# A hybrid GLA/convolution layer whose seven-product matmuls are queued in one line: weights of two products ahead, another product order, two sums accumulated in PSUM

## The chip, the cores and the metric

One Trainium2 chip, one core of it. The metric is the device time of one execution in microseconds (us): median, lowest and highest of several runs. TensorE (PE) multiplies, VectorE (DVE) and ScalarE (ACT) work element by element, SyncE (SP) issues the DMAs; GpSimd (POOL) does next to nothing here.

## The reference, cut to what matters

```python
def hybrid_layer(h, g_pre, w_in, w_gate_up, b_gate, g_gla_out, w_conv, w_out, g_post):
    xn = rmsnorm(h, g_pre)                     # 16 meta tokens + 512, 2048 wide
    p = xn @ w_in
    q, k, v, z_gla, r, hc, gate_b, gate_c, z_conv = jnp.split(p, SPLIT_POINTS, axis=-1)
    log_a = log_sigmoid(r @ w_gate_up + b_gate) / GATE_TAU
    o = gla_chunked(heads(q) * DK ** -0.5, heads(k), heads(v), heads(log_a))   # 4 heads
    y_gla = rmsnorm(o, g_gla_out) * silu(z_gla)
    y_conv = gate_b * causal_dwconv(gate_c * hc, w_conv) * silu(z_conv)
    y = jnp.concatenate([y_gla, y_conv], axis=-1) @ w_out
    return h + rmsnorm(y, g_post)
```

All float32. `gla_chunked` needs, for each head, exponentials of a running sum of `log_a` along the tokens before its own small products can start.

## The kernel before

**Arithmetic.** `x @ w_in` is done with weight tiles of 128 output columns. A float32 operand is split in a high and a low part (`whi`, made by ACT at L117; `wlo = raw - whi`, made by DVE at L118; both in `split`, L113 to L119), and three matmuls, hi by hi, hi by lo and lo by hi, stand for one.

**Pairs and products.** Two weight tiles `na` and `nb` make a pair. Each is loaded in two halves of the 2048 rows: blocks 11 and 12 of `na`, 21 and 22 of `nb`, 512 KB each, into one of five `raw` buffers (`new_raw`, L121; `want`, L143). The 528 tokens are also cut in two halves of 264. The pair is then a 2 by 2 product of blocks, done with seven products P1 to P7 in place of eight (a Strassen-Winograd form). A product is 24 matmuls of 128 by 128 by 256 to 264 into one PSUM bank, written by `make` (L192): the split of its weight block, then the matmuls of L59. The weight blocks of P7, P6, P3 and P5 are sums that DVE makes first (`add`, L190, in place in a raw buffer). The token blocks of P1 to P7 are made once, in the prologue, by `combine` (L462) and `block` (L467 on ACT, L468 on DVE).

There are 25 pairs: z2z3, k1q1, v2v3, z4z5, k2q2, v4v5, z6z7, k3q3, v6v7, and then h0c0, b0s0 to h7c7, b7s7 for the convolution. `pair` (L221) writes one: for each product its split and matmuls, then what takes it out of PSUM, then `step(per)`, which runs some steps of the work in between. It has two forms. The one with `before` (the first three pairs) takes its products from `sums_first` (L202), in the order P7, P5, P6, P1, P2, P3, P4; the sum of P7 goes to one raw buffer more than the four blocks (`s3`, L208). The other uses P1, P2, P7, P6, P3, P5, P4. The results of a pair are sums of products: `q` and `f`, `u`, `v` are copies or partial sums in SBUF (L287, L298 on ACT; L303, L304, L308 on DVE), `put` and L313, L319 write the results.

**Work in between.** Generators queued in `left_over`: for each GLA head `decay` (L545: `log_a` from a small matmul `zp`, then on ACT exp, ln, and six exponentials, on DVE the running sum, L556), `gla_b` (L596), `gla_c` (L632), `gla_d` (L649) and `gla_e` (L670). After each z pair `silu` (L327) runs on ACT and a DMA writes `zd`.

**Stages.** Prologue (loads, `x` split, the plain matmuls of k0, q0, r, v0, v1, z0, z1; L345 to L507), in which the token blocks are made as their source tokens come free, and where the first five products of z2z3 are asked for (`got`, L497 to L506); the nine pairs with the GLA work; the 16 pairs of the convolution (L710); and the output product with norm and residual (L746 to L821).

**What sets the order.** The program text is not the order on an engine: a scheduler puts each engine's instructions in a fixed list when the kernel is built, and each engine works its list in order. Names such as `z2z3P` in the profile are PSUM banks of a pair's products. `ident`, `tpk`, `tpm` and `tpv` belong to small transposes of the GLA stage `gla_b`.

Of the kernel before, what the change touches and what calls it, by code (L numbers as in the profile page):

```python
# [41 lines left out]
def hymba_kernel(ctx, tc, xT, x, g_pre, w_r, w_t, w_up, b_gate, g_gla, w_conv, w_o, g_post, out):  # L42
# [98 lines left out]
    raws = {}  # L141

    def want(name):  # L143

        if name not in raws:
            i = TILE[name]
            raws[name] = []
            for g in range(2):
                r = new_raw()
                nc.sync.dma_start(r, w_t[i][:, NB * g:NB * g + NB, :])  # L150
                raws[name].append(r)

# [39 lines left out]
    def make(na, nb, name, raw, w):  # L192
        hi, lo = split(raw, [P, NB, P])
        (xh, xl), s = xc[name]
        pt = bank(f"{na}{nb}{name}")[:, 0:w]
        for k in range(NB):
            mm(pt, hi[:, k, :], xh[:, s, k, XHALF - w:], k == 0, False)
            mm(pt, hi[:, k, :], xl[:, s, k, XHALF - w:], False, False)
            mm(pt, lo[:, k, :], xh[:, s, k, XHALF - w:], False, k == NB - 1)
        return pt  # L200

    def sums_first(na, nb, w):  # L202

        want(na)
        want(nb)
        a11, a12 = raws.pop(na)
        a21, a22 = raws.pop(nb)
        s3 = new_raw()  # L208
        V.tensor_tensor(out=s3, in0=a11, in1=a21, op=ALU.add)
        yield make(na, nb, "P7", s3, w)  # L210
        add(a21, a22)
        yield make(na, nb, "P5", a21, w)
        add(s3, a22)
        yield make(na, nb, "P6", s3, w)
        yield make(na, nb, "P1", a11, w)
        yield make(na, nb, "P2", a12, w)
        add(a12, s3)
        yield make(na, nb, "P3", a12, w)
        yield make(na, nb, "P4", a22, w)

    def pair(na, nb, c0, dst_a, dst_b, nxt=(), stages=(), per=2, before=None, got=()):  # L221


        w = XHALF - c0

        def tmp(name):
            return ev.tile([P, XHALF], F32, name=name)[:, 0:w]

        def put(dst, in0, in1, op):
# [3 lines left out]
        if before is not None:  # L233
            left_over.extend(before)
            seq, got = got if got else (sums_first(na, nb, w), [])
            got = list(got)

            def get():
                return got.pop(0) if got else next(seq)

            p = get()
            u = tmp("u")
            A.copy(u, p)
            step(per)
            p = get()
            f = tmp("f")
            A.copy(f, p)
            step(per)
            p = get()
            v = tmp("v")  # L250
            V.tensor_tensor(out=v, in0=p, in1=u, op=ALU.subtract)
            step(1000)
            left_over.extend(stages)
            dst_a, dst_b = dst_a(), dst_b()
            p = get()
            q = tmp("q")
            A.copy(q, p)
            V.tensor_tensor(out=v, in0=v, in1=q, op=ALU.subtract)
            add(u, v)
            add(u, f)  # L260
            put(dst_b[1], v, f, ALU.add)
            step(per)
            p = get()
            put(dst_a[0], p, q, ALU.add)
            step(per)
            p = get()
            put(dst_a[1], p, u, ALU.subtract)
            step(per)
            for n in nxt:
                want(n)  # L270
            p = get()
            put(dst_b[0], v, p, ALU.subtract)
            step(1000)
            return

        left_over.extend(stages)
        want(na)
        want(nb)
        a11, a12 = raws.pop(na)
        a21, a22 = raws.pop(nb)  # L280

        def product(name, raw):
            return make(na, nb, name, raw, w)

        p = product("P1", a11)
        q = tmp("q")
        A.copy(q, p)  # L287
        step(per)
        p = product("P2", a12)
        dst_a, dst_b = dst_a(), dst_b()  # L290
        put(dst_a[0], p, q, ALU.add)
        step(per)
        for n in nxt:
            want(n)
        add(a11, a21)
        p = product("P7", a11)
        v = tmp("v")
        A.copy(v, p)  # L298
        step(per)
        add(a11, a22)  # L300
        p = product("P6", a11)
        u = tmp("u")
        V.tensor_tensor(out=u, in0=p, in1=q, op=ALU.subtract)  # L303
        V.tensor_tensor(out=v, in0=u, in1=v, op=ALU.subtract)  # L304
        step(per)
        add(a12, a11)
        p = product("P3", a12)
        V.tensor_tensor(out=u, in0=p, in1=u, op=ALU.subtract)  # L308
        step(per)
        add(a21, a22)  # L310
        p = product("P5", a21)
        for o, s, e in dst_a[1]:
            V.tensor_tensor(out=o, in0=u[:, s - c0:e - c0], in1=p[:, s - c0:e - c0],  # L313
                            op=ALU.subtract)
        put(dst_b[1], p, v, ALU.add)
        step(per)
        p = product("P4", a22)
        for o, s, e in dst_b[0]:
            V.tensor_tensor(out=o, in0=v[:, s - c0:e - c0], in1=p[:, s - c0:e - c0],  # L319
                            op=ALU.subtract)  # L320
        step(1000)
# [363 lines left out]
    def k_q(h, nxt, *stages, **kw):  # L685
        pair(f"k{h}", f"q{h}", 0, lambda: new_k(h), lambda: new_q(h), nxt, stages, **kw)

    def v_v(h, nxt, *stages, **kw):
        pair(f"v{2 * h}", f"v{2 * h + 1}", 0, lambda: new_v(2 * h), lambda: new_v(2 * h + 1), nxt,
             stages, **kw)  # L690

    def z_z(h, nxt, *stages, **kw):
        pair(f"z{2 * h}", f"z{2 * h + 1}", NM // 2, lambda: new_z(2 * h), lambda: new_z(2 * h + 1),
             nxt, stages, **kw)
        silu(2 * h, 2 * h + 1)
# [6 lines left out]
    v_v(2, ("z6", "z7"), gla_e(1), decay(2))
    z_z(3, ("k3", "q3"), gla_b(2), gla_c(2), gla_d(2))
    k_q(3, ("v6", "v7"), gla_e(2))
    v_v(3, ("h0", "c0"), decay(3))


    ycat = {}

    def conv(j, nxt, *stages):  # L710
        hh = g1.tile([P, L], F32, tag="kn", name="hh")[:, 0:S + 2]
        cc = g1.tile([P, L], F32, tag="qn", name="cc")[:, 0:S + 2]
        c0 = NM // 2 - 2

        def two(t):
            return ([(t[:, 0:S // 2 + 2], c0, XHALF)], [(t[:, S // 2 + 2:], NM // 2, XHALF)])

        pair(f"h{j}", f"c{j}", c0, lambda: two(hh), lambda: two(cc), (f"b{j}", f"s{j}"), stages[0])
        V.tensor_tensor(out=hh, in0=hh, in1=cc, op=ALU.mult)
        y = g1.tile([P, L], F32, tag="rr", name="y")[:, 0:S]  # L720
        A.activation(y, hh[:, 0:S], AF.Copy, scale=wc[:, j, 0:1])
        for i in (1, 2):
            V.scalar_tensor_tensor(out=y, in0=hh[:, i:i + S], scalar=wc[:, j, i:i + 1], in1=y,
                                   op0=ALU.mult, op1=ALU.add)
        bb = g1.tile([P, L], F32, tag="vt0", name="bb")[:, 0:S]
# [148 lines left out]
```

## Time and profile before

| | us |
|---|---|
| median of 3 runs | 852.63 |
| lowest, highest | 852.21, 853.37 |
| profiled execution, its own time | 851.39 |
| its span | 849.4 |
| PE busy in the span | 811.0 (95%) |
| DVE busy | 636.5 (75%) |
| ACT busy | 386.7 (46%) |
| mean granted PE clock | 0.985 |

The span is the time from the first to the last instruction that the profiler saw on the core; the profiled execution's own time is 2.0 us longer. Busy times of different engines overlap. A value in square brackets in a timeline row is how long the engine had been idle before that instruction, with what it waited for.

### The profile page before, as it was taken

What the parts mean: (1) busy time and instruction counts of PE and PEld (TensorE: products, weight loads), DVE (VectorE), ACT (ScalarE), POOL (GpSimd) and SP (SyncE); (2) the same over time, 40 slices, a digit from 0 to 9 for tenths busy, and PEclk for the clock granted to TensorE, in tenths of its full rate; (3) what the DMA queues carried; (4) which work ended last, traced back from release to release, by engine and by line L of the source; (5) the groups of instructions that cost most, each with busy time, mean ns of one, the idle gap of its engine ahead of it and who ended that gap; (6) DMA issues with size and microseconds to landing.
All of it is one profiled execution on the core that took longest, in us unless ns stands there. A gap on an engine that the chain in (4) does not pass through costs nothing.

```text
span 849.4 us, 14218 instructions
## 1 busy us (share of the span) xinstructions
PE 811.0 (95%) x5980; PEld 768.2 (90%) x5980; DVE 636.5 (75%) x823; ACT 386.7 (46%) x524; POOL 2.3 (0%) x14
## 2 busy tenths in 40 slices
PE   8999696998989999999999999999999899999996
PEld 8999696998989999999999999999999688888886
DVE  6999778789889889988888888888888814050433
ACT  7635463476473665444444444444444723140411
POOL 0000000000000000000000000000000000000000
PEclk9999898998999999999999999999999999999998
DMA  9522141323322351363332233333333615050154
GB/s 297 197 71 67 63 149 51 123 76 100 100 100 100 106 158 60 100 221 102 100 100 100 100 120 107 122 105 122 118 104 116 246 61 197 1 199 0 50 189 159
DMA packets 30560, 98.92 MB, mean 116 GB/s; under 512 B 3904, under 2 KB 4800, under 8 KB 29728
## 3 DMA queue, kind: packets, MB, share of 16 engines
q1 hardware_dynamic: 28912, 94.86, 33.8%
q10 hardware_dynamic: 1584, 3.15, 1.0%
q8 instruction: 47, 0.77, 0.4%
q14 instruction: 17, 0.14, 0.0%
HBM read 89.61 MB, written 8.39 MB: 115 GB/s over the span
## 4 chain that ended last, share of the span: by engine, by line
PE 80%; DVE 9%; ACT 7%; issue 2%; DMA 2%; SPq 0%; DVEq 0%; ACTq 0%
PE out L59 21%; PE v L59 3%; PE z L59 3%; PE z2z3P L59 2%; PE v2v3P L59 2%; PE h7c7P L59 2%; PE h5c5P L59 2%; PE h2c2P L59 2%; PE h6c6P L59 2%; PE h4c4P L59 2%; PE h3c3P L59 2%; PE h1c1P L59 2%; PE b3s3P L59 2%; PE b6s6P L59 2%; PE b5s5P L59 2%
## 5 line engine op out<-in xcount | busy, mean ns | idle before, releaser
L117 ACT CAST whi<-raw 128x1024 fp32r<-128x1024 f32 x207 | 216.5, 1050 | 231.8 <-DVE raw L190 47.5
L118 DVE TENSOR_TENSOR wlo<-raw,whi 128x1024 fp32r<-128x1024 f32 x207 | 250.7, 1221 | 46.2 <-ACT whi L117 45.8
L190 DVE TENSOR_TENSOR raw<-raw 128x1024 f32<-128x1024 f32 x97 | 118.3, 1221 | 2.9 <-DMA raw<-in_w_t_dram 1.4
L800 DVE TENSOR_TENSOR yg<-out,gpost 128x512 f32<-128x512 f32 (+1 forms) x17 | 11.2, 659 | 107.1 <-ACT junk L799 106.9
L799 ACT ACTIVATE junk<-out 128x512 f32<-128x512 f32 (+1 forms) x17 | 9.7, 572 | 117.5 <-PE out L59 117.5
L59 PE MATMUL out<-whi,ygh 128*128 128x512 f32 (+1 forms) x136 | 51.5, 382 | 2.5 <-ACT ygh L754 2.5
L59 PE MATMUL out<-whi,ygl 128*128 128x512 f32 (+1 forms) x136 | 52.0, 382 | 0.3 <-DVE ygl L755 0.3
L59 PE MATMUL out<-wlo,ygh 128*128 128x512 f32 (+1 forms) x136 | 51.9, 381 | 0.0
L59 PE MATMUL out<-whi,ych 128*128 128x512 f32 (+1 forms) x136 | 51.9, 381 | 0.0
L59 PE MATMUL out<-whi,ycl 128*128 128x512 f32 (+1 forms) x136 | 51.9, 381 | 0.0
L59 PE MATMUL out<-wlo,ych 128*128 128x512 f32 (+1 forms) x136 | 51.9, 381 | 0.0
L59 PEld LDWEIGHTS out<-whi,ygh 128*128 128x128 f32 x136 | 25.4, 188 | 8.1 <-ACT ygh L754 2.7
L59 PEld LDWEIGHTS out<-whi,ygl 128*128 128x128 f32 x136 | 25.5, 187 | 6.2 <-DVE ygl L755 0.8
L59 PEld LDWEIGHTS out<-wlo,ych 128*128 128x128 f32 x136 | 25.5, 188 | 5.5
L59 PEld LDWEIGHTS out<-wlo,ygh 128*128 128x128 f32 x136 | 25.5, 187 | 5.5
L59 PEld LDWEIGHTS out<-whi,ycl 128*128 128x128 f32 x136 | 25.5, 188 | 5.5
L59 PEld LDWEIGHTS out<-whi,ych 128*128 128x128 f32 x136 | 25.5, 187 | 5.5
L128 ACT CAST whi<-raw 128x1024 fp32r<-128x1024 f32 (+2 forms) x13 | 10.9, 845 | 20.4 <-PE v L59 9.6
L59 PE MATMUL z2z3P<-xt,whi 128*128 128x256 f32 x48 | 10.5, 318 | 7.5 <-ACT whi L117 7.5
L59 PEld LDWEIGHTS z2z3P<-xt,whi 128*128 128x128 f32 x48 | 8.7, 220 | 8.0 <-ACT whi L117 8.0
L59 PE MATMUL k1q1P<-xb,whi 128*128 128x264 f32 x32 | 7.2, 324 | 7.1 <-ACT whi L117 7.1
L59 PEld LDWEIGHTS k1q1P<-xb,whi 128*128 128x128 f32 x32 | 6.0, 226 | 7.3 <-ACT whi L117 7.3
(687 smaller groups left out, 2336.4 us busy)
## 6 DMA issues: line engine op xcount, KB each, us to landing
raw<-in_w_t_dram SPq DMA_DIRECT2D x108, 512.0 KB, 4.3
raw<-in_w_o_dram SPq DMA_DIRECT2D x32, 512.0 KB, 5.0
xres<-in_x_dram SPq DMA_DIRECT2D x4, 1024.0 KB, 6.1
xr<-in_xT_dram SPq DMA_DIRECT2D x7, 528.0 KB, 6.5
z<-zd SPq DMA_DIRECT2D x8, 256.0 KB, 3.2
yd<-z SPq DMA_DIRECT2D x8, 256.0 KB, 2.2
yg<-yd SPq DMA_DIRECT2D x1, 2048.0 KB, 9.6
out_dram<-yg SPq DMA_DIRECT2D x8, 256.0 KB, 2.5
```

The lines of the kernel that those rows point to most:

```text
L59: nc.tensor.matmul(out_, lhsT, rhs, start=start, stop=stop)
L117: A.copy(hi, raw)
L118: V.tensor_tensor(out=lo, in0=raw, in1=hi.bitcast(F32), op=ALU.subtract)
L128: A.copy(hi[:, k, :], raw[:, k, :])
L190: V.tensor_tensor(out=a, in0=a, in1=b, op=ALU.add)
L799: nc.scalar.activation(junk, pt, AF.Square, accum_out=s_)
L800: nc.vector.tensor_tensor(out=yg[:, t, cs], in0=pt, in1=gpost[:, cs], op=ALU.mult)
```

## The change

All 25 pairs are entered in one list, `line`, of 175 products, by a class `Pair`. Each product has three parts: `prepare` (the sum, the split, the loads of the next pair's blocks), `multiply` (the 24 matmuls) and `away` (what takes it out of PSUM). A loop at the end of the text prepares up to two products ahead of the one that it multiplies. The order is P5, P1, P6, P2, P3, P7, P4 for all pairs. P2 is added onto P1's bank and P3 onto P5's, by matmuls that go on accumulating, so that the bank name of P2's matmuls is now P1's, and that of P3's is P5's. ACT's copies `q` (of P1) and `f` (of P5) are taken before that; one result half is then copied by ACT (L265). The signs of some sums of blocks change, and P7's weight block is a difference (L213). No pair uses a fifth raw buffer any more. In the prologue the blocks are made in another order, and the first three products of z2z3 are multiplied between them. The GLA stages start at other products (`STAGE`, the letters d, t, s, o, g for `decay` and `gla_b` to `gla_e`): those in `stages` are queued when a pair's P2 is taken away, those in `before` at its P5.

```diff
-ORDER = ("P1", "P2", "P7", "P6", "P3", "P5", "P4")
+ORDER = ("P5", "P1", "P6", "P2", "P3", "P7", "P4")
+AHEAD = 2
...
+        def prepare(self, name, nxt):
+            for b in ("21", "22", "11", "12"):
+                self.load(b)
+            raw = self.raw
+            if name == "P5":
+                add(raw["21"], raw["22"])
+            elif name == "P6":
+                add(raw["11"], raw["21"])
+            elif name == "P3":
+                add(raw["12"], raw["11"])
+            elif name == "P7":
+                V.tensor_tensor(out=raw["11"], in0=raw["11"], in1=raw["22"], op=ALU.subtract)
+            b = {"P5": "21", "P1": "11", "P6": "11", "P2": "12", "P3": "12", "P7": "11",
+                 "P4": "22"}[name]
+            two = split(raw[b], [P, NB, P])
+            if nxt and name in ("P5", "P6", "P4"):
+                nxt.load({"P5": "21", "P6": "22", "P4": "11"}[name])
+                if name == "P4":
+                    nxt.load("12")
+            return two
+
+        def multiply(self, name, two):
...
+            bank_of = {"P2": "P1", "P3": "P5"}.get(name)
+            if bank_of:
+                pt = self.sb[bank_of]
...
+        def away(self, name):
+            sb = self.sb
+            if name == "P5":
+
+                left_over.extend(STAGE[g[0]](int(g[1])) for g in self.before)
+                A.copy(self.tmp("f"), sb["P5"])
+            elif name == "P1":
+
+                A.copy(self.tmp("q"), sb["P1"])
+            elif name == "P6":
+                V.tensor_tensor(out=self.tmp("u"), in0=sb["P6"], in1=sb["q"], op=ALU.subtract)
+            elif name == "P2":
...
+                left_over.extend(STAGE[g[0]](int(g[1])) for g in self.stages)
+                self.dst_a, self.dst_b = self.dst()
+                for o, s, e in self.dst_a[0]:
+                    A.copy(o, sb["P1"][:, s - self.c0:e - self.c0])
+            elif name == "P3":
+                self.put(self.dst_a[1], sb["P5"], sb["u"], ALU.subtract)
+            elif name == "P7":
+                v = self.tmp("v")
+                V.tensor_tensor(out=v, in0=sb["u"], in1=sb["P7"], op=ALU.subtract)
+                self.put(self.dst_b[1], v, sb["f"], ALU.subtract)
+            else:
+                self.put(self.dst_b[0], sb["v"], sb["P4"], ALU.subtract)
...
-    z_z(2, ("k2", "q2"), gla_e(0), decay(1))
-    k_q(2, ("v4", "v5"), gla_b(1), gla_c(1), gla_d(1))
...
+        z_z(2, stages=("g0", "d1"), per=3)
+        k_q(2, stages=("t1", "s1", "o1"), per=3)
...
-        order = sums_first("z2", "z3", XHALF - NM // 2)
-        got = [next(order)]
+        all_pairs()
+        prepare_next()
+        prepare_next()
         block("P1", xa, 0, b11)
-        got.append(next(order))
+        multiply(0)
+        prepare_next()
         block("P2", xb, 0, b21)
...
+    for n in range(len(line)):
+        while len(ready) < min(len(line), n + 1 + AHEAD):
+            prepare_next()
+        if n >= first:
+            multiply(n)
+        away(n)
```

Three places of the engines' lists. **DVE at the end of the prologue.** L402 (now L440) scales the last z tile; L468 (L506) makes low parts of token blocks; L209 and L190 (L183) make sums of weight blocks, L118 (L119) their low parts. Before:

```order
L402 TENSOR_TENSOR raw_886<-z10_901,rstd_109 128x256
L402 TENSOR_TENSOR raw_886<-z11_902,rstd_109 128x256
L468 TENSOR_TENSOR xb1_100<-xr_108,xb0_99 128x1056 x2
L209 TENSOR_TENSOR raw_1013<-raw_1005,raw_1009 128x1024
L190 TENSOR_TENSOR raw_1009<-raw_1009,raw_1011 128x1024
L118 TENSOR_TENSOR wlo_1016<-raw_1013,whi_1015 128x1024
L118 TENSOR_TENSOR wlo_1050<-raw_1009,whi_1049 128x1024
```

And of the change, where raw_1005 is the sum for P5, raw_1009 P1's block and then P6's sum, raw_1011 P2's block and then P3's sum:

```order
L183 TENSOR_TENSOR raw_1005<-raw_1005,raw_1007 128x1024
L506 TENSOR_TENSOR xa1_98<-tt_521,xa0_97 128x1056
L506 TENSOR_TENSOR xa1_98<-xr_108,xa0_97 128x1056
L119 TENSOR_TENSOR wlo_1015<-raw_1005,whi_1014 128x1024
L119 TENSOR_TENSOR wlo_1021<-raw_1009,whi_1020 128x1024
L506 TENSOR_TENSOR xb1_100<-xr_108,xb0_99 128x1056
L440 TENSOR_TENSOR raw_886<-z10_901,rstd_109 128x256
L440 TENSOR_TENSOR raw_886<-z11_902,rstd_109 128x256
L183 TENSOR_TENSOR raw_1009<-raw_1009,raw_1005 128x1024
...
L119 TENSOR_TENSOR wlo_1055<-raw_1009,whi_1054 128x1024
...
L183 TENSOR_TENSOR raw_1011<-raw_1011,raw_1009 128x1024
...
L119 TENSOR_TENSOR wlo_1124<-raw_1011,whi_1123 128x1024
```

The first sum and two low parts have moved ahead of the last z tile; before, the first sum came behind it and behind all the token blocks. (The rows left out are L506 behind raw_1009's sum; the low part of P2, wlo_1090, and L506 twice behind wlo_1055; and L506 behind raw_1011's sum.)

**PE, third to fifth product of z2z3** (change; whi_1054 is P6's weight block, whi_1123 P3's, whi_1089 P2's):

```order
L60 MATMUL z2z3P6_1093<-xt0_766,wlo_1055 128x256
L60 MATMUL z2z3P5_1028<-xb0_99,whi_1123 128x256
L60 MATMUL z2z3P5_1028<-xb1_100,whi_1123 128x256
L60 MATMUL z2z3P1_1064<-xb0_99,whi_1089 128x256
L60 MATMUL z2z3P1_1064<-xb1_100,whi_1089 128x256
L60 MATMUL z2z3P1_1064<-xb0_99,wlo_1090 128x256
```

Two matmuls of P3 stand ahead of all of P2; P3's other 22 follow P2.

**ACT in the decay of head 1.** Before (whi_2104 and whi_2140 are the weights of z4z5's P5 and P4, whi_2174 that of k2q2's P1):

```order
L554 ACTIVATE esx_1968<-esx_1968 128x528
L117 CAST whi_2104<-raw_1852 128x1024
L117 CAST whi_2140<-raw_1854 128x1024
L578 ACT_TABLE_LOAD
L578 ACTIVATE dec_2022<-B_1967 128x4
L573 ACTIVATE eqk_1969<-eqk_1969 128x512
L574 ACTIVATE eqk_1969<-eqk_1969,lns_76 128x512
L577 ACTIVATE esx_1968<-esx_1968 128x528
L575 ACTIVATE esx_1968<-esx_1968 128x512
L580 ACTIVATE B_1967<-B_1967,lns_76 128x512
L117 CAST whi_2174<-raw_1982 128x1024
```

And of the change (whi_2123 is k2q2's P1, whi_2166 its P6; z_2005 and z_2006 are z4 and z5, whose silu (L330) stood behind the whole decay before; ahead of these rows stand the two biased exps of L591, a table load, the exp of L595, the cast of k2q2's P5, a table load and the ln of L596):

```order
L300 ACT_TABLE_LOAD
L300 ACTIVATE z_2005<-z_2005 128x512
L118 CAST whi_2123<-raw_2041 128x1024
L620 ACT_TABLE_LOAD
L620 ACTIVATE dec_2074<-B_2026 128x4
...
L622 ACTIVATE B_2026<-B_2026,lns_76 128x512
L253 COPY f_2197<-k2q2P5_2172 128x264
L300 ACT_TABLE_LOAD
L300 ACTIVATE z_2006<-z_2006 128x512
L567 CAST ed0_2157<-B_2026 128x512
L256 COPY q_2228<-k2q2P1_2203 128x264
L118 CAST whi_2166<-raw_2041 128x1024
```

(Between the rows of L620 and L622 stand the same four exponentials as before, in another order.) Behind the exponentials stood the weights of k2q2's first product, P1; now those of its first two, P5 and P1, stand among them and those of its third, P6, behind, and the silu of z4 and of z5 has moved into the chain, each with a table load. The copy `q` of P1's bank stands ahead of P6's weights.

## Rows read from the trace of the kernel before

**Rows 1.** The page: share and count of busy time by engine; the 40 slices of PE and of the clock granted to it; shares of the chain that ended last by engine; the load of a weight block with its median time from issue to landing.

```profile
PE 811.0 (95%) x5980; PEld 768.2 (90%) x5980; DVE 636.5 (75%) x823; ACT 386.7 (46%) x524; POOL 2.3 (0%) x14
...
PE   8999696998989999999999999999999899999996
...
PEclk9999898998999999999999999999999999999998
...
PE 80%; DVE 9%; ACT 7%; issue 2%; DMA 2%; SPq 0%; DVEq 0%; ACTq 0%
...
raw<-in_w_t_dram SPq DMA_DIRECT2D x108, 512.0 KB, 4.3
```

**Rows 2.** The view of stretches, all engines: start and end in us, length, then busy us and (instructions) of PE, PEld, DVE, ACT and POOL, the granted clock, the DMA share and GB/s.

```profile
86.00:116.00 30.00, 22.50 (x175) 22.00 (x174) 24.04 (x27) 13.23 (x16) 0.53 (x1) 0.89 0.25 86
116.00:146.00 30.00, 22.47 (x169) 21.74 (x168) 22.86 (x36) 18.46 (x26) 0.00 (x0) 0.89 0.33 99
146.00:190.00 44.00, 44.00 (x366) 43.13 (x366) 35.81 (x53) 25.08 (x41) 0.00 (x0) 1.00 0.29 97
190.00:201.00 11.00, 6.65 (x37) 6.22 (x37) 9.86 (x18) 6.47 (x13) 0.00 (x0) 0.69 0.27 77
...
250.00:256.00 6.00, 3.14 (x22) 2.38 (x22) 6.00 (x14) 4.63 (x8) 0.00 (x0) 1.00 0.04 15
...
325.00:328.00 3.00, 1.38 (x12) 1.09 (x11) 3.00 (x6) 1.92 (x3) 0.00 (x0) 1.00 0.03 5
...
363.00:365.00 2.00, 0.74 (x7) 0.54 (x7) 1.86 (x6) 1.61 (x3) 0.00 (x0) 1.00 0.29 72
...
380.00:659.00 279.00, 279.00 (x2351) 279.00 (x2349) 238.98 (x286) 121.14 (x141) 0.00 (x0) 1.00 0.34 110
```

**Rows 3.** The waits of PE: what waited, for whom, total us, how often, the longest us.

```profile
PE z2z3P L59 <- ACT whi L117: 7.5, 2, 7.0
PE k1q1P L59 <- ACT whi L117: 7.1, 1, 7.1
PE k2q2P L59 <- ACT whi L117: 4.3, 1, 4.3
PE out L59 <- ACT ygh L754: 2.5, 1, 2.5
PE v6v7P L59 <- DVE wlo L118: 1.6, 1, 1.6
PE z6z7P L59 <- ACT whi L117: 1.5, 1, 1.5
PE v4v5P L59 <- DVE wlo L118: 1.4, 1, 1.4
PE ot L678 <- DVE on L665: 1.3, 1, 1.3
```

**Rows 4.** The view of stretches again (columns as in rows 2): the first microseconds of PE behind its three longest idle times, and one behind the wait of 2.5 us.

```profile
93.40:97.30 3.90, 3.38 (x14) 3.09 (x15) 3.62 (x4) 1.20 (x2) 0.00 (x0) 0.50 0.07 23
138.30:142.00 3.70, 3.55 (x14) 3.25 (x15) 3.40 (x3) 0.90 (x1) 0.00 (x0) 0.50 0.69 239
195.00:200.00 5.00, 4.96 (x23) 4.73 (x24) 4.79 (x6) 1.52 (x4) 0.00 (x0) 0.50 0.43 113
...
662.00:663.00 1.00, 0.96 (x4) 0.43 (x3) 1.00 (x2) 1.00 (x2) 0.00 (x0) 1.00 1.02 430
```

**Rows 5.** The timeline of DVE at the end of the prologue: start, us, line, operation, count, idle time before.

```profile
75.50 0.75 DVE L402 TENSOR_TENSOR raw<-z,rstd 128x256 f32<-128x256 f32 x2
76.16 2.42 DVE L462 TENSOR_TENSOR tt<-tt,xr 128x1056 f32<-128x1056 f32 x2
...
86.98 0.75 DVE L402 TENSOR_TENSOR raw<-z,rstd 128x256 f32<-128x256 f32 x2
87.65 2.42 DVE L468 TENSOR_TENSOR xb<-xr,xb 128x1056 fp32r<-128x1056 f32 x2
91.04 1.22 DVE L209 TENSOR_TENSOR raw<-raw 128x1024 f32<-128x1024 f32 x1 [0.98 <-DMA zd<-raw]
```

**Rows 6.** The timeline of ACT in the decay of head 1, columns as in rows 5.

```profile
181.74 0.85 ACT L549 ACTIVATE esx<-zp,bg 128x264 f32<-128x264 f32 x2
...
183.54 1.28 ACT L553 ACT_TABLE_LOAD   x1
184.84 0.65 ACT L553 ACTIVATE esx<-esx 128x528 f32<-128x528 f32 x1
185.39 0.35 ACT L298 COPY v<-z4z5P 128x256 f32<-128x256 f32 x1
...
191.67 0.72 ACT L574 ACTIVATE eqk<-eqk,lns 128x512 f32<-128x512 f32 x1
...
197.59 0.61 ACT L525 CAST ed<-B 128x512 fp32r<-128x512 f32 x1
```

**Rows 7.** Groups of instructions by line and form between 380 and 659 us: count, busy us, mean ns of one, idle time before them.

```profile
L118 DVE TENSOR_TENSOR wlo<-raw,whi 128x1024 fp32r<-128x1024 f32 x98 | 118.6, 1221 | 19.2 <-ACT whi L117 19.1
L304 DVE TENSOR_TENSOR v<-u,v 128x258 f32<-128x258 f32 x7 | 3.0, 429 | 0.7
...
L117 ACT CAST whi<-raw 128x1024 fp32r<-128x1024 f32 x98 | 103.1, 1052 | 136.7 <-DVE raw L190 18.6 <-PE h1c1P L59 8.5 <-PE b2s2P L59 8.4
L287 ACT COPY q<-h1c1P 128x258 f32<-128x258 f32 x1 | 0.4, 378 | 0.0
```

**Rows 8.** The chain that ended last, one pair of the convolution: start, us, what.

```profile
399.81 19.90 PE b1s1P L59 x168
```

More of the change, by code (lines that the diff above doesn't have):

```diff
@@ L139, in load_gran @@
         return gran
[L141 to L151, printed above, removed]
     def plain_k(pts, wt, kt, c0):
@@ L177, in hymba_kernel @@
     left_over = []
+    STAGE = {}
+    line = []
+    ready = []
     def step(n):
@@ L190, in add @@
         V.tensor_tensor(out=a, in0=a, in1=b, op=ALU.add)
[L192 to L229, printed above, removed]
+    class Pair:
+        def __init__(self, na, nb, c0, dst, done=None, stages=(), before=(), per=2):
+            self.na, self.nb, self.c0, self.w, self.dst = na, nb, c0, XHALF - c0, dst
+            self.done, self.stages, self.before, self.per = done, stages, before, per
+            self.raw, self.sb = {}, {}
+            for n, name in enumerate(ORDER):
+                line.append((self, n, name))
+        def load(self, b):
+            if b not in self.raw:
+                r = new_raw()
+                g = NB * (b in ("12", "22"))
+                i = TILE[self.na if b[0] == "1" else self.nb]
+                nc.sync.dma_start(r, w_t[i][:, g:g + NB, :])
+                self.raw[b] = r
+        def prepare(self, name, nxt):
[19 more added lines that the diff above has]
+        def multiply(self, name, two):
+            hi, lo = two
+            (xh, xl), s = xc[name]
+            c0, w = self.c0, self.w
+            bank_of = {"P2": "P1", "P3": "P5"}.get(name)
+            if bank_of:
+                pt = self.sb[bank_of]
+            else:
+                pt = bank(f"{self.na}{self.nb}{name}")[:, 0:w]
+                self.sb[name] = pt
+            kw = {"skip_group_check": True} if bank_of else {}
+            for k in range(NB):
+                mm(pt, hi[:, k, :], xh[:, s, k, c0:], k == 0 and not bank_of, False, **kw)
+                mm(pt, hi[:, k, :], xl[:, s, k, c0:], False, False, **kw)
+                mm(pt, lo[:, k, :], xh[:, s, k, c0:], False, k == NB - 1, **kw)
+        def tmp(self, name):
+            self.sb[name] = ev.tile([P, XHALF], F32, name=name)[:, 0:self.w]
+            return self.sb[name]
+        def put(self, dst, in0, in1, op):
+            c0 = self.c0
@@ L230, in put @@
             for o, s, e in dst:
                 V.tensor_tensor(out=o, in0=in0[:, s - c0:e - c0], in1=in1[:, s - c0:e - c0], op=op)
[L233 to L321, printed above, removed]
+        def away(self, name):
[8 more added lines that the diff above has]
+            elif name == "P2":
+                if self.before:
+                    step(1000)
+                left_over.extend(STAGE[g[0]](int(g[1])) for g in self.stages)
[8 more added lines that the diff above has]
+                self.put(self.dst_b[1], v, sb["f"], ALU.subtract)
+            else:
+                self.put(self.dst_b[0], sb["v"], sb["P4"], ALU.subtract)
@@ new lines, in prepare_next, with multiply, away @@
+    def prepare_next():
+        n = len(ready)
+        if n < len(line):
+            p, i, name = line[n]
+            at = line.index((p, 0, ORDER[0])) + len(ORDER)
+            ready.append(p.prepare(name, line[at][0] if at < len(line) else None))
+    def multiply(n):
+        p, i, name = line[n]
+        p.multiply(name, ready[n])
+    def away(n):
+        p, i, name = line[n]
+        p.away(name)
+        step(p.per if i < len(ORDER) - 1 else 1000)
+        if i == len(ORDER) - 1 and p.done:
+            p.done()
@@ L683, in gla_e @@
             yield
[L685 to L695, printed above, removed]
@@ L697, in hymba_kernel @@
-    z_z(1, ("k1", "q1"), before=(), got=(order, got))
-    k_q(1, ("v2", "v3"), before=(decay(0),), per=3)
-    v_v(1, ("z4", "z5"), gla_c(0), gla_d(0), before=(gla_b(0),))
-    z_z(2, ("k2", "q2"), gla_e(0), decay(1))
-    k_q(2, ("v4", "v5"), gla_b(1), gla_c(1), gla_d(1))
[L702 to L725, printed above, removed]
-        sg = g1.tile([P, L], F32, tag="vt1", name="sg")[:, 0:S]
-        pair(f"b{j}", f"s{j}", NM // 2, lambda: main_only(bb), lambda: main_only(sg), nxt, stages[1])
-        A.activation(sg, sg, AF.Silu)
-        V.tensor_tensor(out=y, in0=y, in1=bb, op=ALU.mult)
-        return y, sg
@@ L732, in conv_end @@
[L732 to L743 removed]
+    STAGE.update(d=decay, t=gla_b, s=gla_c, o=gla_d, g=gla_e)
```

90 lines of the change are left out of this document (67 added, 23 removed).

## The prediction, made before the changed kernel was run

> **What bounds the kernel now.** I read the page first: PE is busy for 811.0 of 849.4 us, and 80% of the chain that ended last is PE [rows 1]. So the end moves only by PE's idle time and by time at a low clock. The slices (21.2 us each) show where these are: the PE line falls to 6 in the fifth and seventh, to 8 in the tenth and twelfth, and the clock line falls to 8 in the fifth, seventh and tenth [rows 1]. The view of stretches gives sizes [rows 2]: PE is idle for 7.5 us in 86 to 116, 7.5 in 116 to 146, 4.35 in 190 to 201, 2.9 in 250 to 256, 1.6 in 325 to 328, 1.3 in 363 to 365; nothing in 146 to 190, and nothing at all in 380 to 659, the convolution, where DVE is busy for 239 of 279 us and never the limit. The waits name the cause [rows 3]: the first product of z2z3 waits for its weights behind the last z tile; k1q1, k2q2, v4v5 with z6z7, and v6v7 wait for weights which stand behind the decay of heads 0 to 3 in the lists of ACT and DVE. The last look is at the clock [rows 4]: behind the idle times of 7.0, 7.1 and 4.3 us TensorE ran at 1.2 GHz (0.50) for busy times of 3.38, 3.55 and 4.96 us, and half of each is lost against 2.4 GHz: 1.7 + 1.8 + 2.5 = 6.0 us. Behind the 2.5 us in front of the output product it stayed at 1.00 [rows 4].
>
> Before, the idle time that the change can touch is therefore 7.5 + 7.5 + 4.35 + 2.9 + 1.6 + 1.3 = 25.15 us, and 6.0 of clock: 31.2.
>
> **The change, part by part.** I walk each engine's list with durations of the rows. A product is 19.90 / 7 = 2.85 us of PE [rows 8]; a low part or a sum 1.22, pitched some 1.15 apart where they follow each other (two token blocks take 2.42) [rows 5, 7]; a cast 1.05, a copy out of PSUM 0.38 [rows 7].
>
> *Head.* Before, the first sum starts at 91.04, behind four token blocks, the z tile and a wait for the DMA that empties a buffer which it takes as fifth one [rows 5]; PE waits until 93.40 [rows 4]. Now the sum is made in place and stands two token blocks behind the two combines at 76.16 [rows 5]. From there six large instructions and some 0.8 us of waits for ACT's blocks give 84, and P5's low part 85: before the z matmuls end at 93.40 - 7.0 = 86.4 [rows 3, 4]. P5 and P1 start without a wait. DVE goes on: P1's low part to 86.1, a block, the z tile (0.75) to 88.0, P6's sum to 89.1, a block, P6's low part to 91.4; P6 is due at 86.4 + 5.7 = 92.1. Behind it PE's list has two matmuls of P3, ahead of P2. P3's sum comes behind P2's low part and two blocks, at 96.1, its cast at 97.2; P6 ends at 94.95. **A wait of 2.25 remains** of 7.5 + 1.7.
>
> *Decay of head 1.* The `zp` matmuls start the chain; ACT's list is then: two biased exps 0.74, table load 1.28, exp 0.65, cast 1.03, load 1.28, ln 0.65, load 1.28 and silu 0.63, cast 1.04, load 1.28, `dec`, the four exponentials and `B` 3.24, copy 0.37, load 1.28 and silu 0.63, `ed` 0.61, copy 0.37, cast of P6 1.04 [rows 6, 7]: 17.4, with a little DVE time 17.6. PE has five products ready behind `zp`: P3, P7, P4, then P5 and P1 of k2q2, 14.25 us. **Wait 3.4** where 4.35 and 2.5 of clock stood.
>
> *Decays of heads 2 and 3.* No silu stands in these chains, which come to 13.5; but the copy `q` of P1's bank stands ahead of P6's cast, so P6 cannot start before P1's end + 0.38 + 1.05 = 1.4. With the low part and the next block's cast behind it I get **2.8 and 2.75**, where 2.9 and 1.6 stood: nothing gained, 1.1 lost.
>
> *Decay of head 0.* It starts one product later than the others in its pair's order. The cast of v2v3's P5 stands at 14.6 + 0.8 (a wait for DVE's scan) behind `zp`, four products and four single matmuls cover 11.9. **Wait 3.5** (part of it ahead of P3's low part), where 7.5 and 1.8 stood.
>
> *Copies, sums in PSUM.* DVE loses some 50 instructions, about 0.4 us each [rows 7], ACT gains 23. In the convolution PE had no idle time [rows 2], so that is worth nothing there; it is hidden by PE. Without this cover it would be 20 us of DVE. Matmuls that add to a used bank are as many as before, of the same shape: 0. Gain or loss from them is bounded by nothing shown, except that in-bank accumulation is what all but the first of the 24 matmuls do already.
>
> *Bank.* P2 may write P1's bank only once ACT has copied `q`. P6 (2.85) lies between, the copy takes 0.38: ACT may be late by 2.4 before PE waits. *Loads.* The next pair's fourth block to be needed first is asked for at P6 and lands 4.3 us later [rows 1]; the next P5 is prepared three products, 8.5 us, after. Hidden.
>
> *A rule against the change.* ACT's next instruction starts 1.30 us after the table load's start (183.54, 184.84), and the copy at 185.39 overlaps the end of the exp [rows 6]: a switch costs its own row. The change puts two more switches into head 1's chain. The Trainium skill, "ScalarE: Activation LUTs", section "What ACT_TABLE_LOAD costs", says that a switch costs some 1380 ns of drain besides the 1283 ns load, and to keep functions of one set together. By that, five loads would make the chain 6.9 us longer and head 1's wait 10.3; the trace shows the load of 1.28 and no drain, so the sum goes by the row.
>
> **Sum.** After: 2.25 + 3.5 + 3.4 + 2.8 + 2.75 + 1.3 (`ot`, as before) = 16.0 us, and no low clock, since the longest single waits are about 3.4 us. For these the rows only say: 2.5 without a drop, 4.3 with one. I take no drop, because each is nearer to the first in kind (one short wait), but it is close; a drop costs 1.7 to 2.5 each. Gain 31.2 - 16.0 = 15.2, less 0.3 for rounding of small waits: 14.9. The profiled execution was 851.39, the median is 852.63, 1.24 higher. 851.39 - 14.9 = 836.5; + 1.24 = **837.7 us**.
>
> **Rivals.**
> - *Only the floor remains* (0.10). If the decay chains run as in rows but the casts are not late beyond the floor of 1.4 each, the four decays cost 5.6 in place of 12.45: 830.8. For it: my walk adds each small DVE wait. Against: head 1's two silus.
> - *Low clock behind each decay* (0.14). Four waits of about 3 us, each followed by 2.0 us lost: 837.7 + 8 = 845.7. For it: 4.3 us was enough before. Against: 2.5 was not.
> - *Switches hold ACT longer than their row* (0.02). Twice the row for each of the five loads: 5 x 1.28 = 6.4 on head 1's wait, then 9.8, with 2.5 of clock: 846.6. The page named above would have it so; rows 6 do not.
> - *The look-ahead does not reach past the decay: slower* (0.05). If the weights of the next pair's P5 and P1 also came behind the whole chain, only three products, 8.55, would cover 17.4 + 2.1 of ACT: 10.9 us of wait in each of four decays, with 2.0 of clock, 51.6 in place of 20.7 (7.5 + 1.8 + 4.35 + 2.5 + 2.9 + 1.6), less 6.95 gained at the head: 852.6 + 24 = 876.6. It decides from waits of 4.9 us each on. For it: an instruction on ACT that waits for DVE or a DMA holds all behind it. Against: both casts stand inside the chain in the list.
> - *The bank takes it back* (0.05). If ACT were late with `q` by 3.0 us in each pair, PE would wait 0.6 in each of 25, 15 us: 852.7. Against: ACT is busy for 121 of 279 us in the convolution [rows 2].
>
> **The numbers.** The forecast gets 0.64. Faster by over 0.2% (1.7 us, what a measurement of this kernel can tell from no change): 0.64 + 0.10 + 0.14 + 0.02 = 0.90; within: 0.05; slower: 0.05. The range reaches to the floor case and past the low-clock case: 830 to 848. Left out are the last two rivals and the tails of the others.
>
> **What would show it.** Right: in 86 to 97 PE's only long wait is some 2 us ahead of the first matmul of P3; k1q1 and k2q2 keep waits of about 3.5 us, the clock stays 1.00 behind them; no idle PE from 365 to the end of the convolution; DVE some 20 us less busy. Wrong: waits of 5 us or more in a decay, 0.50 in the clock behind them, or PE waiting for ACT's copies within pairs of the convolution.

## The result, and the profile after

The changed kernel takes **844.28 us** (median of 4 runs, 842.24 to 845.31) where the kernel before takes 852.76 (4 runs): ratio 0.9897, 95% interval 0.9878 to 0.9917. It is faster by 8.5 us; the forecast was 14.9. The profiled execution is 844.2, its span 842.5.

The page of the changed kernel, the rows that answer to [rows 1]:

```profile
PE 812.3 (96%) x5980; PEld 769.4 (91%) x5980; DVE 621.1 (74%) x770; ACT 394.7 (47%) x547; POOL 2.3 (0%) x14
...
PE   8999898998989998999999999999998999999996
...
PEclk9999999998999999999999999999999999999999
...
PE 82%; DVE 8%; ACT 5%; issue 3%; DMA 2%; SPq 0%; DVEq 0%; ACTq 0%
```

DVE is 15.4 us less busy, ACT 8.0 more; PE's digits in the fifth and seventh slice have risen from 6 to 8. But PE's busy time has risen too, by 1.3 us, with the same number of matmuls: part of its work ran slowly. The slices are too coarse to show it. The stretches and the waits of the changed kernel (columns as in [rows 2] and [rows 3]):

```profile
86.00:104.00 18.00, 15.40 (x120) 15.20 (x119) 17.61 (x18) 9.47 (x13) 0.53 (x1) 0.91 0.30 103
...
123.00:133.00 10.00, 6.61 (x51) 5.86 (x50) 9.89 (x17) 8.82 (x15) 0.00 (x0) 1.00 0.19 54
133.00:191.00 58.00, 58.00 (x484) 57.24 (x483) 48.17 (x69) 34.22 (x52) 0.00 (x0) 1.00 0.35 112
191.00:202.00 11.00, 7.00 (x40) 6.57 (x39) 9.44 (x13) 6.70 (x10) 0.00 (x0) 0.69 0.42 134
...
245.00:253.00 8.00, 4.93 (x39) 4.41 (x39) 7.49 (x12) 5.12 (x10) 0.00 (x0) 1.00 0.15 55
...
319.00:332.00 13.00, 9.58 (x65) 9.06 (x65) 11.81 (x17) 6.51 (x12) 0.00 (x0) 0.87 0.14 40
...
364.00:366.00 2.00, 1.51 (x14) 1.51 (x14) 1.94 (x5) 0.97 (x1) 0.00 (x0) 1.00 0.71 227
366.00:648.00 282.00, 282.00 (x2375) 282.00 (x2374) 235.48 (x263) 126.11 (x156) 0.00 (x0) 1.00 0.35 115
648.00:659.00 11.00, 8.19 (x39) 6.59 (x38) 9.70 (x11) 9.21 (x11) 0.00 (x0) 0.84 0.84 298
```

```profile
PE k2q2P L60 <- ACT whi L118: 4.0, 1, 4.0
PE h0c0P L60 <- ACT whi L118: 2.8, 1, 2.8
PE z2z3P L60 <- ACT f L253: 2.6, 1, 2.6
PE out L60 <- ACT ygh L745: 2.5, 1, 2.5
PE k1q1P L60 <- DVE wlo L119: 1.8, 2, 1.2
PE v2v3P L60 <- ACT whi L118: 1.6, 1, 1.6
PE z6z7P L60 <- ACT whi L118: 1.6, 1, 1.6
PE z6z7P L60 <- DVE wlo L119: 1.5, 1, 1.5
```

Idle time of PE, before and after: head 7.5 and 2.6; decay of head 0 7.5 and 3.4; of head 1 4.35 and 4.0; of head 2 2.9 and 3.1; of head 3 1.6 and 3.4; `ot` 1.3 and 0.5. And the clock behind the waits of 2.5 us and more, to be set beside [rows 4]:

```profile
98.00:101.90 3.90, 3.03 (x14) 3.03 (x15) 3.88 (x5) 1.61 (x4) 0.00 (x0) 0.56 0.20 63
195.50:201.00 5.50, 5.13 (x24) 4.90 (x25) 5.09 (x5) 3.31 (x6) 0.00 (x0) 0.51 0.47 146
325.50:331.00 5.50, 5.36 (x32) 5.25 (x33) 5.10 (x5) 2.95 (x6) 0.00 (x0) 0.69 0.32 95
653.00:658.50 5.50, 4.92 (x13) 3.65 (x14) 5.50 (x6) 5.50 (x7) 0.00 (x0) 0.69 0.99 371
```

All four were followed by work at the lower level of 1.2 GHz (0.50 in single half microseconds, such as 99.0 to 99.5; the stretches above mix in what came after it). Summed by half microseconds, busy time times the missing share of the clock, that is 1.5 + 2.5 + 1.7 + 1.7 = 7.4 us; the same sum over the kernel before gives 6.1. The fourth place is ahead of the output product, where the same wait of 2.5 us [rows 3] had cost no clock in the execution profiled before. So the span's 6.9 us are: 8.8 gained in idle time from the head to the output product (86 to 664 before, 86 to 660 after), 1.3 given back to the clock, 1.3 given back because the matmuls of `v` in the prologue began later in this execution (at 41.45 us in place of 40.11; 39.6 to 40.7 in the profiles of all experiments), and 0.7 gained that I have not placed.

### The profile page after: what moved, and what is told of

Same layout as the page of the kernel before. It is cut to its first block, busy times and chain, and to the rows that moved or that the text cites. A ratio compares the mean times of both kernels' runs of the same rounds, so it can differ in the third digit from the quotient of the medians.

```text
span 842.5 us, 14191 instructions
## 1 busy us (share of the span) xinstructions
PE 812.3 (96%) x5980; PEld 769.4 (91%) x5980; DVE 621.1 (74%) x770; ACT 394.7 (47%) x547; POOL 2.3 (0%) x14
## 4 chain that ended last, share of the span: by engine, by line
PE 82%; DVE 8%; ACT 5%; issue 3%; DMA 2%; SPq 0%; DVEq 0%; ACTq 0%
PE out L60 21%; PE v L60 3%; PE k3q3P L60 2%; PE v2v3P L60 2%; PE h7c7P L60 2%; PE h5c5P L60 2%; PE h2c2P L60 2%; PE h6c6P L60 2%; PE h4c4P L60 2%; PE h3c3P L60 2%; PE h1c1P L60 2%; PE b3s3P L60 2%; PE b6s6P L60 2%; PE b5s5P L60 2%; PE b4s4P L60 2%
## 5 line engine op out<-in xcount | busy, mean ns | idle before, releaser
L118 ACT CAST whi<-raw 128x1024 fp32r<-128x1024 f32 x207 | 216.4, 1051 | 222.7 <-DVE raw L183 94.2
L119 DVE TENSOR_TENSOR wlo<-raw,whi 128x1024 fp32r<-128x1024 f32 x207 | 251.9, 1222 | 49.1 <-ACT whi L118 45.3
L183 DVE TENSOR_TENSOR raw<-raw 128x1024 f32<-128x1024 f32 x75 | 90.1, 1221 | 4.6 <-DMA raw<-in_w_t_dram 3.8
L213 DVE TENSOR_TENSOR raw<-raw 128x1024 f32<-128x1024 f32 x25 | 30.6, 1223 | 0.6
L60 PE MATMUL k2q2P<-xt,whi 128*128 128x264 f32 x48 | 10.3, 315 | 4.0 <-ACT whi L118 4.0
L130 DVE TENSOR_TENSOR wlo<-raw,whi 128x1024 fp32r<-128x1024 f32 (+2 forms) x13 | 12.5, 970 | 0.8 <-ACT whi L129 0.8
L60 PE MATMUL h0c0P<-xt,whi 128*128 128x258 f32 x48 | 10.4, 316 | 2.8 <-ACT whi L118 2.8
```

What stands on the lines that cost most here:

```text
L60: nc.tensor.matmul(out_, lhsT, rhs, start=start, stop=stop, **kw)
L118: A.copy(hi, raw)
L119: V.tensor_tensor(out=lo, in0=raw, in1=hi.bitcast(F32), op=ALU.subtract)
L130: V.tensor_tensor(out=lo[:, k, :], in0=raw[:, k, :], in1=hi[:, k, :].bitcast(F32), op=ALU.subtract)
L183: V.tensor_tensor(out=a, in0=a, in1=b, op=ALU.add)
L213: V.tensor_tensor(out=raw["11"], in0=raw["11"], in1=raw["22"], op=ALU.subtract)
```

## The experiments

The theory after the result: the waits came out as walked, and what is missing is the clock behind waits too short to be feared. "Unchanged" below is the changed kernel, 844.28. "Lost to the clock" is summed as above, and is that of one execution. The experiments were measured at other times than the changed kernel, and the median of the kernel before lay between 852.30 and 853.46 there; a difference of less than some 1 us between two kernels shows nothing.

**1. Work in the waits.**

```diff
+    def fill(n):
+        src = xc["P1"][0][0]
+        with tc.issue_after(...):          # behind the matmul before it
+            pt = bank("fill")
+            for k in range(n):
+                mm(pt[:, 0:XHALF], src[:, 0, k % NB, 0:P], src[:, 0, k % NB, :], True, True)
```

> The changed kernel with extra matmuls of token blocks by token blocks into a bank nobody reads (16 ahead of P2 of z2z3, 24 ahead of P6 of k2q2, 16 ahead of P6 of h0c0, 16 ahead of the output product), so that TensorE works during its four longest waits. Theory (the missing part of the gain is TensorE at 1.2 GHz behind waits of 2.5 to 4.0 us): the waits stay, the granted clock stays at 1.00 behind them, 6 to 7 us come back: 837.5. Rival 1 (the low clock comes from something else than those waits, so it stays): 844 to 845. Rival 2 (the extra matmuls themselves delay the products by as much as the clock gives back): 842 to 846.

Measured 839.20 (838.02 to 839.80; ratio to before 0.9834, 0.9819 to 0.9849). The three places in its pairs and the output product, as above:

```profile
86.00:104.00 18.00, 17.34 (x146) 17.13 (x145) 17.66 (x18) 9.45 (x13) 0.53 (x1) 1.00 0.34 114
...
190.00:202.00 12.00, 10.75 (x87) 10.26 (x87) 11.06 (x14) 6.08 (x10) 0.00 (x0) 1.00 0.34 111
...
318.00:332.00 14.00, 13.18 (x111) 12.86 (x110) 12.32 (x16) 7.17 (x12) 0.00 (x0) 1.00 0.27 75
648.00:659.00 11.00, 10.04 (x42) 7.83 (x43) 10.69 (x11) 9.36 (x10) 0.00 (x0) 1.00 0.64 249
```

In the profile the clock is 1.00 at the four places and nothing is lost to it; 72 matmuls more, 5.1 us less. This is the theory's side, some 2 us short of the clock's 7.4. The places where they stand account for that, so rival 2 is right in part. At P6 of k2q2, where PE had waited 4.0, the new timeline has

```profile
187.30 0.39 PE L60 MATMUL k2q2P<-xa,wlo 128*128 128x264 f32 x1 [0.90 <-DVE wlo L129]
190.07 3.06 PE L60 MATMUL fill<-xa 128*128 128x264 f32 x24
193.94 0.51 PE L60 MATMUL k2q2P<-xt,whi 128*128 128x264 f32 x2 [0.81 <-ACT whi L128]
194.89 0.51 PE L60 MATMUL k2q2P<-xb,whi 128*128 128x264 f32 x2 [0.44 <-ACT whi L128]
```

which is 5.2 us of waits and extra matmuls; at the head, in h0c0 and ahead of the output product it is 2.8, 2.9 and 3.2 where 2.6, 2.8 and 2.5 stood, together 2.2 more. The record also lists each execution's mean granted clock: 0.998 in two of the four (838.02, the profiled one, and 838.80) and 0.995 in the two slower ones, so that in these something was lost to the clock again.

**2. The same in the kernel before.** 50 such matmuls ahead of the first product of z2z3, 50 ahead of P3 of k1q1.

> The kernel before with extra matmuls (50 ahead of the first product of z2z3, 50 ahead of P3 of k1q1) in its two longest waits, lists of ACT and DVE as before but for six rows. Theory (1.85 + 1.76 us of its time are low clock behind those two waits): 852.7 - 3.6 = 849.1. Rival (the low clock only moves to the next wait, or the extra matmuls cost as much): 852 to 853.

Measured 851.07 (849.40 to 853.28, 12 runs; 0.9976, 0.9964 to 0.9988), between the two. In its profile 6.3 us are lost to the clock, no less than without: the place behind 138 us is gone, but z2z3 had low clock again behind two later waits of 0.9 and 0.8, and the wait ahead of the output product, harmless in the profile before, now cost 1.6. Extra work that leaves a short wait behind it may or may not keep the clock: the rests of 0.7 to 1.1 us in the profile of experiment 1 were followed by no drop.

**3. The head.** The wait of 2.6 us in z2z3. ACT's and PE's timelines in the changed kernel:

```profile
97.50 1.04 ACT L118 CAST whi<-raw 128x1024 fp32r<-128x1024 f32 x1 [5.02 <-DVE raw L183]
98.45 0.36 ACT L253 COPY f<-z2z3P 128x256 f32<-128x256 f32 x1
98.72 0.38 ACT L256 COPY q<-z2z3P 128x256 f32<-128x256 f32 x1
```

```profile
98.87 1.22 PE L60 MATMUL z2z3P<-xb,whi 128*128 128x256 f32 x4 [2.60 <-ACT f L253]
```

P3's cast ended as far behind P6 as walked, but P3 adds onto P5's bank, and the copy `f` that has to leave it stands behind that same cast. First P3 was held behind P2 on PE:

```diff
+        if n == 4:
+            with tc.issue_after(...):      # P2's last matmul
+                p.multiply(name, ready[n])
```

> The changed kernel with P3 of z2z3 held behind P2 in TensorE's order. Theory (the wait at the head is only the two matmuls of P3 that stand ahead of P2): wait 2.6 falls to about 0.5, no low clock behind it: 844.3 - 2.1 - 1.5 = 840.7. Rival (P2 would have waited as long, for its own token blocks or for the copy q): 844.

Measured 842.76 (839.55 to 843.71). The rival was right on the wait:

```profile
PE z2z3P L60 <- ACT q L258: 2.9, 1, 2.9
```

P2 adds onto P1's bank, and `q` stands behind the cast as `f` does. So the copies were put first, by preparing P3's weights after them:

```diff
         block("P3", xb, 1, b22)
-        prepare_next()
         block("P4", xa, 1, tt)
```

> The changed kernel with the weights of P3 of z2z3 prepared after the copies f and q, so that ACT takes the copies ahead of P3's cast. Theory (P2, held behind P3 only in the list, waited in the second run above for the copy q, which stood behind P3's cast): head's wait 2.6 to 0.7 or less, no low clock: 844.3 - 1.9 - 1.5 = 840.9. Rival (DVE's sum of P3, now behind u, makes P3 wait 2 us or more in place of P2): 843 to 844.

Measured 840.72 (839.27 to 841.50; 0.9859, 0.9842 to 0.9875): 3.6 us less.

```profile
PE z2z3P L60 <- ACT whi L118: 0.8, 1, 0.8
PE z2z3P L60 <- ACT q L256: 0.8, 1, 0.8
```

The wait fell to 1.6 in two pieces, with no drop behind them: 1.0 and 1.5 of the 3.6, the rest is not placed. The bank's reuse was the head's price, though not in the way that my rival had it: not the copy's 0.38, but its place in ACT's list.

**4. The fifth buffer.**

```diff
+            if name == "P5" and self.na == "z2":
+                s5 = new_raw()
+                V.tensor_tensor(out=s5, in0=raw["21"], in1=raw["22"], op=ALU.add)
```

> The changed kernel with the sum of P5 of z2z3 alone put into a fifth raw buffer, as the kernel before did for its first product. Theory (that buffer, which the last z tile's DMA has to leave, is what put the first sum behind the token blocks): P5 waits for about 7 us, low clock behind it, in place of 2.6 and 1.5: 844.3 + 5 = 849.3. Rival (the new order of blocks in the prologue made the gain at the head): no wait of over 3 us ahead of P5, 844 to 845.

Measured 847.80 (846.72 to 851.32), 3.5 more. Wait and DVE timeline are those of the kernel before [rows 3, 5]:

```profile
PE z2z3P L60 <- ACT whi L118: 7.1, 2, 7.0
```

```profile
91.15 1.23 DVE L208 TENSOR_TENSOR raw<-raw 128x1024 f32<-128x1024 f32 x1 [0.97 <-DMA zd<-raw]
```

So the old head came from that buffer, and the new order of blocks alone does not remove it.

**5. Look-ahead.** `AHEAD = 0`.

> The changed kernel with AHEAD = 0: each product's weights are written in the program right before its matmuls, as in the kernel before. Theory 1 (the look-ahead of two products covers the decays): without it 5.7 us less cover in each of four decays and low clock behind each: 860 or more. Theory 2 (the lists are made by what is ready, so that the text's look-ahead hardly matters, and the order of products and the places of the GLA stages do): within 4 us of 844.3; decays 2 and 3, whose casts then stand ahead of the copy q, 1.4 us shorter each: 841.

Measured 846.98 (845.78 to 847.99), 2.7 more: theory 2 in kind, but its second part (decays 2 and 3 shorter) was wrong.

```profile
PE h0c0P L60 <- DVE wlo L119: 4.2, 1, 4.2
...
PE z6z7P L60 <- DVE wlo L119: 3.7, 1, 3.7
```

The casts did move ahead of `q`, but DVE's low part of P1 moved behind the decay's multiplications, and PE waited for that within P1. For h0c0, in the changed kernel and here:

```profile
318.72 1.22 DVE L119 TENSOR_TENSOR wlo<-raw,whi 128x1024 fp32r<-128x1024 f32 x1
...
324.71 1.22 DVE L119 TENSOR_TENSOR wlo<-raw,whi 128x1024 fp32r<-128x1024 f32 x1
```

In the traces ACT's order differs in 14 of 547 rows and DVE's in 32 of 770; that fits a scheduler which orders by what is ready.

**6. Sums in PSUM undone.** P2 and P3 in banks of their own, added by DVE.

> The changed kernel with P2 and P3 in banks of their own and DVE adding them (two more passes of DVE a pair, ACT's copy of the result left out). Theory (DVE and ACT are not what limits the convolution; the sums in PSUM are worth nothing there, and little elsewhere): 844.3, within 2. Rival (DVE's list ends last in the decays, so each more pass there costs its 0.4 us, and the low clock comes more often): 846 to 849.

Measured 847.29 (846.33 to 848.37), 3.0 more. The convolution is as fast as in the changed kernel (259.6 us from the first matmul of h1c1 to the first of b7s7 in both profiles); the rival is right about the decays:

```profile
PE k1q1P L60 <- ACT whi L118: 5.4, 1, 5.4
```

k1q1's waits were 1.8 and v2v3's 1.6 above; now k1q1 has one of 5.4 and v2v3 none, followed by 3.2 us lost to the clock.

**7. The silu in head 1's chain.**

```diff
+    def silu_late():
+        with tc.issue_after(casts["k2", "P3"]):
+            silu(4, 5)
```

> The changed kernel with silu of z4 and z5 held on ACT behind the cast of P3 of k2q2, so outside the chain of head 1's decay. Theory 1 (ACT's list makes that wait): the chain is 3.8 us shorter, the wait of 4.0 falls to the floor of about 1.5, no low clock: 844.3 - 2.5 - 2.5 = 839.3. Theory 2 (DVE's list, with the sum of P6 behind all of the decay's multiplications, ends as late): wait 2 to 3, clock open: 840 to 844.

Measured 839.86 (836.86 to 843.17), 4.4 less. The waits fit theory 2, 3.4 in two pieces in place of 4.0:

```profile
PE k2q2P L60 <- ACT whi L121: 1.8, 1, 1.8
...
PE k2q2P L60 <- DVE wlo L122: 1.6, 1, 1.6
```

That is 0.6 of the 4.4. DVE's sum for P6, behind the decay's multiplications, starts as late as before; in the changed kernel and here:

```profile
193.52 1.22 DVE L183 TENSOR_TENSOR raw<-raw 128x1024 f32<-128x1024 f32 x1
...
193.47 1.22 DVE L186 TENSOR_TENSOR raw<-raw 128x1024 f32<-128x1024 f32 x1
```

The profiled execution was the slowest of the five (843.17), with 8.1 us lost to the clock and a mean granted clock of 0.988; the other four have 0.991 to 0.995 on record and take 836.86 to 840.71. So most of the 4.4 goes with the clock. Where those four kept it, and whether the split wait is the reason, no trace shows.

**8. Three together** (3's copies, 7's silu, extra matmuls).

> The changed kernel with three things together: copies ahead of P3's cast at the head, silu of z4 and z5 behind the chain of head 1, and extra matmuls ahead of P6 of k2q2 (12), P6 of h0c0 (16) and the output product (16). Theory (the parts add up: 839.2 with extra matmuls alone, less 1.9 at the head, less 0.6 in k2q2): 836.7. Rival (without extra matmuls at the head and with fewer in k2q2 the low clock returns there): 838.5 to 841.

Measured 835.98 (835.49 to 837.95; 0.9815, 0.9797 to 0.9833): as the theory had it, the shorter waits come on top of experiment 1's gain. The three gains measured apart (3.6, 4.4 and 5.1) do not add up to the 8.3 here, since each holds part of the same loss to the clock. In the profile nothing is lost to it; one of the five executions has a mean granted clock of 0.993 (837.95).

**9. P2 right behind P1.** In the first of these two kernels, z2z3's `q` is taken after P2 was added, so that pair's numbers differ.

```diff
-ORDER = ("P5", "P1", "P6", "P2", "P3", "P7", "P4")
+ORDER = ("P5", "P1", "P2", "P6", "P3", "P7", "P4")
```

> The changed kernel in the order P5, P1, P2, P6, P3, P7, P4: P2, which adds onto P1's bank, is due right after P1, with some 8 to 11 matmuls of P6 in between in TensorE's list. Theory (the copy q takes 0.38 us and those 1.0 to 1.3 us of P6 cover it): within 2 of 844.3. Rival (the bank's reuse needs the whole product between; PE waits 0.6 us or more in each of 25 pairs): 855 to 865.

Measured 840.19 (839.25 to 841.26), 4.1 less: outside the theory's two, on the other side than the rival. The convolution did pay (row of this kernel, between 380 and 640 us; the changed kernel has 260.00 busy for 2190 matmuls there):

```profile
380.00:640.00 260.00, 256.07 (x2126) 253.41 (x2125) 209.59 (x234) 112.65 (x141) 0.00 (x0) 1.00 0.32 102
```

64 matmuls fewer in the same time, 7.6 us: half of it are waits of 0.5 us for a low part in each pair b, the other half shows as no wait. (From the first matmul of h1c1 to the first of b7s7 it is 266.9 us against 259.6.) But k2q2's wait fell to 2.1, h0c0's to 0.7. P2's weights, now due first, need no sum of DVE, and their cast stands ahead of `q` in ACT's list (182.65 and 190.81 us in k2q2); P6's cast had stood behind both. Which of the two made the wait was not separated. With `q` in its place, 7's silu and 16 matmuls ahead of the output product:

> The order of the run before with P2 due right after P1 (all copies q in their place now), with silu of z4 and z5 behind the chain of head 1 and 16 extra matmuls ahead of the output product. Theory (that order takes the floor out of the decays, 839 to 840; the silu takes 1 to 2 us and one low clock, the extra matmuls another low clock of 1.7): 835.5. Rival (the 0.5 us waits in the pairs b and a remaining low clock keep it above the three together): 837 to 839.

Measured 843.45 (840.26 to 844.78): missed, above the rival too. k1q1 and v2v3 wait 3.4 us again where the run before had 1.5; the silu bought nothing (2.2 against 2.1). At the first matmul of h1c1 this kernel stands at 363.4 us, the run before at 360.1 and the three together (8) at 363.5, and its convolution takes 7.2 us more than that of 8. What else made it later up to there stays open. So that order was put only where it pays, in the three pairs behind a decay:

> The three together (copies ahead of P3's cast at the head, silu behind the chain of head 1, 16 extra matmuls ahead of the output product), with the order P5, P1, P2, P6, P3, P7, P4 in the three pairs that follow a decay (k2q2, z6z7, h0c0) alone, and no extra matmuls ahead of their P6. Theory (the order with P2 right behind P1 takes the floor out of the decays and costs 0.4 to 0.5 us a pair only by the bank's reuse, which is paid in three pairs in place of 25): 836.0 - 1.7 (z6z7) - 2.5 (h0c0) + 1.2 = 833. Rival (what the decays save is paid in the pairs behind them, or the low clock returns behind k2q2): 836 to 838.

Measured **831.12** (830.63 to 832.72; 0.9747, 0.9730 to 0.9763), the fastest of all, 13.2 below the changed kernel. In its profile no wait is over 1.8 and nothing is lost to the clock:

```profile
PE k1q1P L61 <- DVE wlo L133: 1.8, 2, 1.3
PE v2v3P L61 <- ACT whi L132: 1.7, 1, 1.7
PE ot L740 <- DVE on L727: 1.6, 1, 1.6
PE z6z7P L61 <- DVE wlo L133: 1.5, 1, 1.5
```

## Why the prediction was right, and where it was not

- **What bounds the kernel**: right. PE idles at the places named. The convolution is full before and after: between 360 and 650 us DVE is busy for 241.6 us in place of 249.0, which bought nothing there. Of the 15.4 us less DVE (some 20 forecast) that is the half.
- **Head**: 2.25 forecast, 2.6 measured. The place was right and so was the distance from P6's end to the cast's end (2.25; both came 1.3 later); the last releaser was the copy `f` behind the cast that I had timed; I had priced the bank only by the copy's length.
- **Decays**: 3.5, 3.4, 2.8, 2.75 forecast; 3.4, 4.0, 3.1, 3.4 measured, 1.4 us more together. The lists walked with durations of the rows before were good to 0.7 us each. For head 1 the term named the wrong engine: with both silus out of the chain (7) the wait lost only 0.6, because DVE's multiplications end as late. In head 3 it was DVE too: not P1's end plus `q` and a cast, my floor of 1.4, but `ed`, which stands ahead of `q` and waited for DVE, so that PE waited 2.8 for P6's cast:

```profile
323.41 0.62 ACT L567 CAST ed<-B 128x512 fp32r<-128x512 f32 x1 [2.69 <-DVE B L633]
```

In head 2 the floor held (1.6). So the sizes of heads 1 and 3 are in part luck.

- **Table loads**: in the changed kernel the ln ahead of silu's load ends at 183.36, the load starts at 183.38 and its activation at 184.67, 1.29 us later, as before. The drain that the Trainium skill, "ScalarE: Activation LUTs", section "What ACT_TABLE_LOAD costs", adds to each switch does not show here: the wait is 4.0, not 10.
- **No low clock**: this is the step that failed. I let every drop go since the new waits are shorter, and gained 6.0 us by that; 7.4 were lost. My rival of low clock behind each decay gave 845.7, with a chance of 0.14, and it is nearer to what happened than the forecast: a drop behind decays 1 and 3, behind the head, and behind the wait for the output product, none behind decays 0 and 2. Those two waits are split, but so is decay 3's (0.7 and 2.8), and in the second kernel of experiment 3 a drop of 1.5 us followed the split waits of decay 0; what decides it is not shown. Idle time at the places that I summed went from 25.2 to 17.0 (16.0 forecast). 844.3 less the 7.4 is 836.9, beside the 837.7 forecast; that this is so close is partly luck, since waits 1.0 longer and a prologue 1.3 later are in it, and other idle time and the unplaced 0.7 us offset them. Experiment 1, with no drop in its profile, is 839.2.
- **Sums in PSUM**: priced at 0, worth 3.0 (6), not in the convolution but in the lists around the decays. **Look-ahead**: 2.7 (5). **Buffer at the head**: 3.5 (4). Each is what undoing one part alone costs, drops of the clock included, so they need not add up to the 8.5 that the change gains.

## What to carry to other kernels

When stalls of the matmul engine are shortened but not removed, count the clock behind the ones that remain as unchanged until a run shows otherwise (6.1 us before, 7.4 after), and try to cover them with matmuls that nobody reads; that cost one short function here and gave 5 us in the changed kernel, 2 in the kernel before. A bank that is added to later is priced by the place of the copy that must leave it in the other engine's list, not by the copy. Order of products can be chosen pair by pair: the order that shortens a stall behind other work cost 7.6 us where there was no such work.

## What the runs showed that I had not expected

A wait of the same length sometimes costs clock and sometimes not. The 2.5 us ahead of the output product cost nothing in the profile of the kernel before, and 1.6 to 1.7 in the profile of every later kernel that kept it; the 2.8 in h0c0 cost 1.7 in the changed kernel and nothing in the profiles of experiment 4 and of the second kernel of experiment 3. Each drop cost 1.5 to 3.2 us. One profile is one draw. Of 48 further executions of the kernel before that the record lists, 25 have a mean granted clock of 0.983 to 0.986 (median 852.2 us; the profiled one, 851.39, has 0.985) and 23 one of 0.979 to 0.982 (median 854.2). So in about half of them some 2 us more are lost than the 6.1 of the profile; at which wait, no trace shows. The number of drops in a profile does not tell how well a kernel repeats: the kernels with none repeat within 1.8 to 2.5 us, experiment 7, with four, within 6.3, but experiments 5 and 6, with five each, within 2.0 to 2.2.
